# Score products of 128 rows through zero-padded low parts, and constants padded to 64-byte steps, in a four-layer float32 kernel

## The chip, the cores and the metric

The kernel runs on one core of one Trainium2 chip. The metric is device time in microseconds of one execution; the median of three runs is given, with the lowest and the highest. A profile of one further execution shows the instructions of every engine: TensorE (PE; its weight loads are PEld), VectorE (DVE), ScalarE (ACT), GpSimd (POOL), and the DMA queue of SyncE (SP).

## The reference

Four layers work on x, 512 positions of 1024 features, in float32. Layer 1 is stick-breaking attention with 16 heads of 64, layer 2 an HGRN2 mixer with 8 heads of 128, each followed by an MLP with squared ReLU of width 4096. The second block has two layers, each with a gated linear attention branch (4 heads) and a differential attention branch (4 heads, two maps of 64 features each). What the change touches are the scores of both kinds of attention:

```python
# layer 1: q, k are normalised per head of 64 features
z = jnp.einsum('bhqd,bhkd->bhqk', q[:, :, t0:t1], k[:, :, :t1]) * scale
...
# second block: two maps m of 64 features each for a head
s = jnp.einsum('bqhmd,bkhmd->bhmqk', qi, k)
p = jax.nn.softmax(jnp.where(mask, s, -jnp.inf), axis=-1)
attn = p[:, :, 0] - lam * p[:, :, 1]
```

Queries come in blocks of 128, and block t sees the keys up to its own end.

## The kernel before

All activations lie transposed, features on the 128 partitions, positions along the free axis: x0 to x7 are the eight 128-feature chunks of x, 512 columns each. A float32 operand of a projection is held in two parts, a high part h rounded to the short format float32r and a low part l = a - h, so a product a*b is three float32r matmuls: h with wh, l with wh, h with wl, all summed in one PSUM bank. xh and xl are the parts of the normalised x, hh and hl those of other activations (attention outputs, the MLP's hidden layer), wh and wl those of a weight tile, split on the chip from raw, which a DMA fills.

A list of jobs (`job_list`) gives the order: the projections of layer 1 pair by pair (query, key, value of two heads at a time), its output projection, the first MLP, the HGRN projections, their output, the second MLP, then the two layers of the second block. A job of kind T (`job_t`, L558) loads a 128-column weight tile eight times as the stationary operand and streams the 512 positions of hh/hl or xh/xl past it: 24 matmuls of 128x512. A job of kind V (`job_v`, L596) has xh or xl stationary and streams the weights: 96 matmuls. `job_pair` (L532) does the last two output chunks of a phase in halves of 256 columns. All matmuls are issued through `pe` (L400).

The order of instructions on each engine is fixed at build time by a planner, the class `Sched` (L62): every operation has a cost in ns, a thread of work has a priority by its job, and the planner lets a model of the four engines run and appends each operation to its engine where the model dispatches it. The matmul costs are the last entry of each tuple given to `pe`. Buffers are slots in pools: an `Alloc` waits in the model until a slot is free. hh and hl have nine slots each, Q twelve, C, S and A three each. A copy may go to ScalarE or VectorE, whichever the model has free first; subtractions and products go to VectorE; the causal selections of layer 1 (L933) go to GpSimd.

Keys and queries of two heads lie on 64 partitions each of one tile. `headnorm` (L819) normalises the tile, splits it into a high part a and a low part l, and builds for the queries two tiles, one for each head, whose 128 rows hold the head's high part and its low part. For the keys it makes two tiles that hold the head's high part twice, (a, b), and keeps l, with the low parts of both heads on their 64 partitions. `scores` (L881) then takes two matmuls for each query block: one of 128 rows, (q high, q low) with (k high, k high), and one of 64 rows, q high with k low, on the partitions of the head. Head 0's high query part lies on partitions 0 to 63 and head 1's on 64 to 127. Query blocks come in three units (`UNITS`, L867): blocks 0 and 2 together (256 and 384 columns), block 3 (512), block 1 (256). There are 32 issues of each unit: 2 heads or maps of 8 pairs in layer 1 and of 4 heads in each of the two layers of the second block. `sb_elem` (L936) and `d_map` (L1272) issue them; `used` (L871) gives the slots back after the sixth issue.

The constants are laid out in the order in which `const` is called. Each starts at a multiple of 32 bytes of its partition: sv (764 bytes), cst, msk, wgk, neg, kc (32 bytes), x0 to x7, xh, xl, mods, gp, lbt, Rt, rtok, lamt, lp (16 bytes), qbd, onr, then raw, wh, wl and the slots. In this layout x, xh, xl, mods, gp, lbt and Rt start 32 bytes past a multiple of 64; qbd, onr, raw, wh, wl and all slots (hh, hl, Q, C, S, A, v) start at one.

Of the kernel before, what the change touches and what calls it, by code (L numbers as in the profile page):

```python
# [9 lines left out]
F32 = mybir.dt.float32  # L10
# [200 lines left out]
def _fsize(ap):  # L211
    n = 1
    for d in ap.shape[1:]:
        n *= d
    return n
# [75 lines left out]
def block_kernel(ctx: ExitStack, tc, xt, blob, ada, crow_d, sv_d, wgk_d, consts_d, masks_d, out):  # L291
# [7 lines left out]
    def const(name, shape, dtype=F32):  # L299
        return cp.tile(list(shape), dtype, name=name)  # L300
# [3 lines left out]
    msk = const("msk", (128, 4, 32), U8)  # L304
    wgk = const("wgk", (128, 2, 256), F32R)
    neg = const("neg", (64, 64))
    kc = const("kc", (128, 8))
    x = [const(f"x{k}", (128, T)) for k in range(NK)]
    xh = [const(f"xh{k}", (128, T), F32R) for k in range(NK)]
    xl = [const(f"xl{k}", (128, T), F32R) for k in range(NK)]  # L310
# [3 lines left out]
    Rt = const("Rt", (128, T))  # L314
    rtok = const("rtok", (128, 4))
    lamt = const("lamt", (128, 2, 4))
    lp = const("lp", (64, 4))
    ident, ones = cst[:, 0], cst[:, 1]
    one = ones[:, 0:1]
    qbd = const("qbd", (128, 8, 2, 64))  # L320
# [28 lines left out]
    def release(h, l):  # L349
        R.free("hh", h)  # L350
        R.free("hl", l)
# [17 lines left out]
    def tt(out, a, b, op):  # L369
        n = _fsize(out)  # L370
        c = [("DVE", n / 0.96 + 69, lambda: V.tensor_tensor(out=out, in0=a, in1=b, op=op))]  # L371
        return Op(c)
# [27 lines left out]
    def pe(mms, nowait=False):  # L400

        def f():
            for o, a, b, st, sp, _ in mms:
                PE.matmul(o, lhsT=a, rhs=b, start=st, stop=sp)  # L404
        return Op([("PE", sum(m[5] for m in mms), f)], nowait)
# [126 lines left out]
    def job_pair(j, banks, half):  # L532

        role = jobs[j][5]
        l = PAIRS[role]
        evs = operand(role)
        R.spawn(last_chunks(l, banks, j * P - 2), j * P - 2)
        ws = [(yield ev_w[half]), None]
        for i in range(2):
            r = slice(256 * i, 256 * i + 256)  # L540
            for c in range(2):
                if ws[c] is None:
                    ws[c] = yield ev_w[half + 1]
                wh, wl = ws[c]
                o = banks[c][:, r]
                ns = 3 + 256 / 2.4
                for k in range(NK):
                    hh, ll = yield evs[k]
                    a, b = wh[:, k * 128:(k + 1) * 128], wl[:, k * 128:(k + 1) * 128]
                    yield pe([(o, a, hh[:, r], k == 0, False, ns), (o, a, ll[:, r], False, False, ns),  # L550
                              (o, b, hh[:, r], False, k == NK - 1, ns)], nowait=k < NK - 1)
                R.set(ev_done[l, c, i])
                if i:
                    R.free("w", ws[c])
        for k in range(NK):
            release(*evs[k].value)

    def job_t(j, bank, half):  # L558
        role = jobs[j][5]
        w = yield ev_w[half]  # L560
        wh, wl = w
        evs = operand(role)
        split = role == ("wout", 1, NK - 1)
        for r in (slice(0, T // 2), slice(T // 2, T)) if split else (slice(0, T),):
            c = bank[:, r]
            ns = 3 + _fsize(c) / 2.4
            for k in range(NK):
                h, l = yield evs[k]
                a, b = wh[:, k * 128:(k + 1) * 128], wl[:, k * 128:(k + 1) * 128]
                yield pe([(c, a, h[:, r], k == 0, False, ns), (c, a, l[:, r], False, False, ns),  # L570
                          (c, b, h[:, r], False, k == NK - 1, ns)], nowait=k < NK - 1)
            if split and r.start == 0:
                R.spawn(evac[role[0]](j, bank, *role[1:]), (j - AHEAD[role[0]]) * P)
        R.free("w", w)
        last = role[0] == "wo" or role[0] == "wout" or role[0] == "w2"
        if last and role[-1] == NK - 1:
            for k in range(NK):
                release(*evs[k].value)
        if split:
            R.set(ev_last)  # L580
        else:
            R.spawn(evac[role[0]](j, bank, *role[1:]), (j - AHEAD[role[0]]) * P)

    def job_lr(j, bank, half):

        wh, _ = w = yield ev_w[half]
        evs = operand(jobs[j][5])
        for k in range(NK):
            h, l = yield evs[k]
            a = wh[:, k * 128:k * 128 + 64]  # L590
            mms = [(bank[0:64], a, h, k == 0, k == NK - 1, 216), (bank[0:32], a[:, 0:32], l, False, False, 216)]
            yield pe(mms if k == 0 else mms[::-1], nowait=k < NK - 1)
        R.free("w", w)
        R.spawn(e_lr(j, bank, *jobs[j][5][1:]), (j - AHEAD["lr"]) * P)

    def job_v(j, banks, half):  # L596
        role = jobs[j][5]
        evs = operand(role)
        evs2 = [ev_x2[role[1], k] for k in range(NK)] if role[0] == "dv" else evs
        m = 2 if role[0] == "dv" else 1  # L600
        for hf in range(0, 4, m):
            ws = [None] * m
            for n in range(4 * m):
                first, kk = n < 2 * m, n % (2 * m)
                if ws[kk // 2] is None:
                    ws[kk // 2] = yield ev_w[half + hf + kk // 2]
                wh, wl = ws[kk // 2]
                k = hf * 2 + kk
                h, l = yield (evs if first else evs2)[k]
                c = slice(kk % 2 * 512, kk % 2 * 512 + 512)  # L610
                a, b = wh[:, c], wl[:, c]
                done = not first and kk % 2
                for t in (0, 1) if first else (2, 3):
                    th, tl = h[:, t * 128:(t + 1) * 128], l[:, t * 128:(t + 1) * 128]
                    yield pe([(banks[t], th, a, k == 0, False, 216), (banks[t], th, b, False, False, 216),
                              (banks[t], tl, a, False, k == NK - 1, 216)], nowait=not done or t < 3)
                if done:
                    R.free("w", ws[kk // 2])
        for t in range(4):
            R.spawn(evac[role[0]](j, banks[t], *role[1:], t), (j - AHEAD[role[0]]) * P + t)  # L620
# [168 lines left out]
    def sums(out, a, w, tag="A"):  # L789

        if in_areas[0]:
            tags = "N", "N"
            h, l = yield Alloc("N", 2, F32R)
        else:
            tags = "C", "S"
            h = yield Alloc("C", dtype=F32R)
            l = yield Alloc("S", dtype=F32R)
        yield copy(h, a, sbuf=True)
        yield tt(l, a, h.bitcast(F32), ALU.subtract)
        if tag:  # L800
            R.free(tag, a)
        yield pe([(out, w, h, True, False, 216), (out, w, l, False, True, 216)])
        R.free(tags[0], h)
        R.free(tags[1], l)

# [13 lines left out]
    def headnorm(src, gain, bias, tag, is_key, done):  # L819

        a, b, l = yield Alloc(tag, 3, F32R)
        sq = yield Alloc("A")
        yield act(sq, src, AF.Square)
        s = yield Alloc("S")
        p = yield Alloc("tp")
        yield from sums(p, sq, bones_r)
        yield act(s, p, AF.Ln, scale=1.0 / 64, bias=EPSC)  # L830
        R.free("tp", p)
        yield act(s, s, AF.Exp, scale=-0.5, bias=bias)
        yield stt(s, src, gain, s, ALU.mult, ALU.mult)
        done()
        yield copy(a, s, sbuf=True)
        yield tt(l, s, a.bitcast(F32), ALU.subtract)
        R.free("S", s)
        top, bot = slice(0, 64), slice(64, 128)
        yield [copy(b[bot], a[bot], sbuf=True), copy(b[top], a[bot] if is_key else l[bot], sbuf=True)]
        yield copy(a[bot], a[top] if is_key else l[top], sbuf=True)  # L840
        if is_key:
            return (a, b), l
        R.free(tag, l)
        return a, b

# [25 lines left out]
    def used(tag, qn, kn):  # L871

        n = left.setdefault(id(qn), [6, qn])
        n[0] -= 1
        if n[0] == 0:
            R.free(tag, *qn, *kn[0], kn[1])

    def width(unit):
        return sum((qb + 1) * 128 for qb, _ in unit)

    def scores(z, qn, kn, hd, unit):  # L881

        q, (kh, kl) = qn[hd], kn
        r = slice(64 * hd, 64 * hd + 64)
        mms = []
        for qb, off in unit:
            n = (qb + 1) * 128
            w = max(n, 256)
            qc = slice(qb * 128, qb * 128 + 128)
            zo = z[:, off:off + w]  # L890
            mms.append((zo, q[:, qc], kh[hd][:, 0:w], True, False, w / 2.4 + 2))
            mms.append((zo, q[r, qc], kl[r, 0:w], False, True, w / 2.4 + 2))
        return pe(mms)

    def to_keys(src, w, tag, exp=False):
# [441 lines left out]

    def g_decay(l, i, glr):
        p = yield Alloc("z")
        yield pe([(p, wgk[:, l, 128 * i:128 * i + 128], glr, True, True, 216)])  # L1340
        bg = col("bgk", 2 * l + i)
        a = yield Alloc("A")
        yield act(a, p, AF.Abs, bias=bg)
# [339 lines left out]
```

## Time and profile before

| | |
|---|---|
| median of 3 runs | 1844.5 us (1840.95 to 1848.59) |
| profiled execution | 1843.46 us, its span 1841.4 us |
| TensorE | 1812.9 us busy (98%), 9421 matmuls |
| VectorE | 1302.5 us busy (71%) |
| ScalarE | 907.6 us busy (49%) |
| GpSimd | 55.3 us busy (3%) |

The span runs from the first instruction to the last. Layer 1's attention takes until some 262 us, its MLP until 660, HGRN until 930, its MLP until 1320, and the second block's two layers the rest. A matmul's row in the profile spans its whole passage through the engine, so that two neighbours overlap; the step from one start to the next one's is what a matmul costs the engine when nothing waits.

### The profile page before, as it was taken

Reading aid. Unit: us, or ns where it says so; the run is one execution under the profiler, and the core shown is the slowest. Engines: PE = TensorE matmul, PEld = TensorE weight load, DVE = VectorE, ACT = ScalarE, POOL = GpSimd, SP = SyncE. Lnnn points to the kernel's source line nnn. Section 1 sums busy time; section 2 is a strip of 40 time slices with the busy share of each in tenths; the row PEclk is TensorE's granted clock in tenths of the full one; section 3 lists DMA queues with packets and bytes.
Section 4 is the critical chain, followed back from the end, with each engine's and each line's share of the span. In section 5 each row is a group of like instructions: output and inputs, shape, how many; then the busy total and the mean of one; then the engine's idle time right before and its main releaser. Section 6 shows DMA issues by size and latency. Waiting matters only on the chain.

```text
span 1841.4 us, 24301 instructions
## 1 busy us (share of the span) xinstructions
PE 1812.9 (98%) x9421; PEld 1424.6 (77%) x9421; DVE 1302.5 (71%) x2213; ACT 907.6 (49%) x1636; POOL 55.3 (3%) x109
## 2 busy tenths in 40 slices
PE   9999999999999999898999999999999999999999
PEld 6777678888888887676778888888877778877877
DVE  7888877986444569889965353535678886698883
ACT  5778764212222337677742122212458774377771
POOL 0212220000000000000000000000000000000000
PEclk9999999999999999899999999999999999999999
DMA  5111114894222221211222322232222122222122
GB/s 169 61 54 48 57 39 172 300 319 162 96 92 95 100 92 47 70 63 54 69 93 91 102 94 91 95 100 92 92 69 81 58 69 91 92 70 69 58 69 80
DMA packets 49843, 175.53 MB, mean 95 GB/s; under 512 B 5536, under 2 KB 6304, under 8 KB 49728
## 3 DMA queue, kind: packets, MB, share of 16 engines
q1 hardware_dynamic: 49728, 173.99, 28.2%
q8 instruction: 73, 1.20, 0.3%
q14 instruction: 42, 0.34, 0.1%
HBM read 171.87 MB, written 2.10 MB: 94 GB/s over the span
## 4 chain that ended last, share of the span: by engine, by line
PE 90%; DVE 5%; issue 4%; ACT 1%; POOL 0%; POOLq 0%; DVEq 0%
PE bank L404 88%; PE bank L413 2%; DVE wl L371 1%; DVE C L396 1%; DVE S L371 0%; DVE S L376 0%; DVE Q L396 0%; DVE C L371 0%; DVE Q L371 0%; DVE v L376 0%; ACT A L367 0%; ACT big L387 0%; DVE hl L371 0%; DVE xl L376 0%; POOL S L933 0%
## 5 line engine op out<-in xcount | busy, mean ns | idle before, releaser
L404 PE MATMUL bank<-xh,wh 128*128 128x512 f32 (+1 forms) x1296 | 530.3, 409 | 2.2 <-ACT xh L367 1.6
L404 PE MATMUL bank<-xl,wh 128*128 128x512 f32 (+1 forms) x1296 | 513.0, 396 | 0.0
L404 PE MATMUL bank<-xh,wl 128*128 128x512 f32 x1280 | 507.3, 396 | 0.4 <-DVE wl L371 0.4
L371 DVE TENSOR_TENSOR wl<-raw,wh 128x1024 fp32r<-128x1024 f32 (+1 forms) x273 | 332.6, 1218 | 19.5 <-ACT wh L387 15.8
L387 ACT CAST wh<-raw 128x1024 fp32r<-128x1024 f32 x160 | 168.0, 1050 | 342.0 <-PE bank L404 301.8
L404 PE MATMUL bank<-hh,wh 128*128 128x512 f32 (+1 forms) x808 | 308.0, 381 | 2.3 <-DVE hh L389 1.4
L404 PE MATMUL bank<-hh,wl 128*128 128x512 f32 (+1 forms) x808 | 306.3, 379 | 1.6 <-DVE wl L371 1.6
L404 PE MATMUL bank<-hl,wh 128*128 128x512 f32 (+1 forms) x808 | 306.2, 379 | 0.2 <-DVE hl L371 0.2
L404 PEld LDWEIGHTS bank<-xh,wh 128*128 128x128 f32 (+1 forms) x1296 | 243.3, 188 | 69.0 <-issue 8.2
L404 PEld LDWEIGHTS bank<-xh,wl 128*128 128x128 f32 x1280 | 240.8, 188 | 60.4 <-DVE wl L371 2.1
L404 PEld LDWEIGHTS bank<-xl,wh 128*128 128x128 f32 (+1 forms) x1296 | 243.2, 188 | 53.2 <-DVE xl L376 1.2
L371 DVE TENSOR_TENSOR x<-x,bank 128x512 f32<-128x512 f32 (+1 forms) x82 | 55.2, 674 | 183.0 <-PE bank L404 182.6
L404 PEld LDWEIGHTS bank<-hh,wh 128*128 128x128 f32 x808 | 152.0, 188 | 32.0 <-DVE hh L389 1.8
L404 PEld LDWEIGHTS bank<-hh,wl 128*128 128x128 f32 x808 | 152.0, 188 | 31.1 <-DVE wl L371 2.4
L404 PEld LDWEIGHTS bank<-hl,wh 128*128 128x128 f32 x808 | 152.0, 188 | 28.8 <-DVE hl L371 0.5
L367 ACT ACTIVATE S<-A 128x512 f32<-128x512 f32 x64 | 40.5, 633 | 259.7 <-DVE A L376 259.6
L376 DVE SCALAR_TENSOR_TENSOR A<-bank,Rt 128x512 f32<-128x512 f32 x64 | 44.2, 691 | 122.9 <-PE bank L404 122.7
L367 ACT ACTIVATE A<-A 128x512 f32<-128x512 f32 (+1 forms) x220 | 126.9, 595 | 1.7
L389 DVE CAST wh<-raw 128x1024 fp32r<-128x1024 f32 (+1 forms) x115 | 77.8, 677 | 37.6 <-PE bank L404 31.9
L404 PE MATMUL bank<-Q,Q 64*128 64x256 f32 (+5 forms) x256 | 91.2, 407 | 0.0
L404 PEld LDWEIGHTS bank<-Q,Q 128*128 128x128 f32 (+1 forms) x256 | 47.4, 185 | 37.8 <-issue 24.0
L404 PE MATMUL bank<-big,v 128*64 128x128 f32 (+4 forms) x544 | 67.9, 306 | 2.2 <-ACT big L387 2.1
(208 smaller groups left out, 2152.0 us busy)
## 6 DMA issues: line engine op xcount, KB each, us to landing
raw<-blob SPq DMA_DIRECT2D x273, 512.0 KB, 3.5
big<-ada SPq DMA_DIRECT2D x48, 512.0 KB, 4.7
x<-xt SPq DMA_DIRECT2D x8, 256.0 KB, 6.9
out<-x SPq DMA_DIRECT2D x7, 256.0 KB, 2.0
raw<-blob SPq DMA_DIRECT2D x2, 256.0 KB, 4.7
big<-crow SPq DMA_DIRECT2D x1, 512.0 KB, 4.7
out<-x SPq DMA_DIRECT2D x2, 128.0 KB, 1.7
cst<-consts SPq DMA_DIRECT2D x1, 128.0 KB, 6.4
```

The costliest lines, as they stand in the source:

```text
L367: return Op([("ACT", d, lambda: S.activation(out=out, in_=in_, func=func, scale=scale, bias=bias, **kw))])
L371: c = [("DVE", n / 0.96 + 69, lambda: V.tensor_tensor(out=out, in0=a, in1=b, op=op))]
L376: lambda: V.scalar_tensor_tensor(out=out, in0=a, scalar=s, in1=b, op0=op0, op1=op1))])
L387: c.append(("ACT", 0.833 * n + (51 if in_.space == PSUM else 93), lambda: S.copy(out, in_)))
L389: c.append(("DVE", n / (1.92 if sbuf else 0.96) + 68, lambda: V.tensor_copy(out, in_)))
L396: V.tensor_tensor_scan(out=o, data0=one.to_broadcast(list(i.shape)), data1=i, initial=0.0, op0=ALU.mult, op1=ALU.add)
L404: PE.matmul(o, lhsT=a, rhs=b, start=st, stop=sp)
L413: PE.transpose(p[:, b * 128:(b + 1) * 128], src[:, b * 128:(b + 1) * 128], ident)
```

## The change

Keys: `headnorm` takes an hh slot and an hl slot at its start, and GpSimd clears partitions 64 to 127 of the one and 0 to 63 of the other. The subtraction that made l on 128 partitions becomes two on 64 partitions each, one into each slot, so that each holds one head's low part and zeros on the other head's partitions. The two high tiles (a, b) are made as before, but their slots are taken after the norm. `scores` uses the padded slots with the whole 128-row query tile for both matmuls; the zeros take away the query's low part and leave q high with k low. `used` gives the hh and hl slots back. Queries are built as before.

Constants: kc grows from 32 to 64 bytes, lp from 16 to 64. Rt, x, xh, xl, mods, gp and lbt move by 32 bytes, to multiples of 64, and what lies behind lp moves by 64.

Planner: the cost of a matmul is N/2.4 + 13 ns instead of N/2.4 + 3 (or + 2 in the scores), 227 instead of 216 where it is a number. The diff, without the repeated changes of that number:

```diff
-    kc = const("kc", (128, 8))
+
+    kc = const("kc", (128, 16))
...
-    lp = const("lp", (64, 4))
+    lp = const("lp", (64, 16))
...
-                ns = 3 + 256 / 2.4
+                ns = 13 + 256 / 2.4
...
-            ns = 3 + _fsize(c) / 2.4
+            ns = 13 + _fsize(c) / 2.4
...
-        yield pe([(out, w, h, True, False, 216), (out, w, l, False, True, 216)])
+        yield pe([(out, w, h, True, False, 227), (out, w, l, False, True, 227)])
...
-        a, b, l = yield Alloc(tag, 3, F32R)
+        top, bot = slice(0, 64), slice(64, 128)
+        if is_key:
+            ls = []
+            for t_, z_ in (("hh", bot), ("hl", top)):
+                ls.append((yield Alloc(t_, dtype=F32R)))
+                yield Op([("POOL", 460.0, lambda o=ls[-1][z_]: G.memset(o.bitcast(F32), 0.0))], True)
         sq = yield Alloc("A")
...
         done()
+        if is_key:
+            a, b = yield Alloc(tag, 2, F32R)
+            yield copy(a, s, sbuf=True)
+            yield [tt(l[r], s[r], a[r].bitcast(F32), ALU.subtract) for l, r in zip(ls, (top, bot))] + [
+                copy(b[r], a[bot], sbuf=True) for r in (top, bot)]
+            R.free("S", s)
+            yield copy(a[bot], a[top], sbuf=True)
+            return (a, b), tuple(ls)
+        a, b, l = yield Alloc(tag, 3, F32R)
         yield copy(a, s, sbuf=True)
         yield tt(l, s, a.bitcast(F32), ALU.subtract)
         R.free("S", s)
-        top, bot = slice(0, 64), slice(64, 128)
-        yield [copy(b[bot], a[bot], sbuf=True), copy(b[top], a[bot] if is_key else l[bot], sbuf=True)]
-        yield copy(a[bot], a[top] if is_key else l[top], sbuf=True)
-        if is_key:
-            return (a, b), l
+        yield [copy(b[bot], a[bot], sbuf=True), copy(b[top], l[bot], sbuf=True)]
+        yield copy(a[bot], l[top], sbuf=True)
...
-            R.free(tag, *qn, *kn[0], kn[1])
+            R.free(tag, *qn, *kn[0])
+            release(*kn[1])
...
-        q, (kh, kl) = qn[hd], kn
-        r = slice(64 * hd, 64 * hd + 64)
+        q, kh, kl = qn[hd], kn[0][hd], kn[1][hd]
...
-            mms.append((zo, q[:, qc], kh[hd][:, 0:w], True, False, w / 2.4 + 2))
-            mms.append((zo, q[r, qc], kl[r, 0:w], False, True, w / 2.4 + 2))
+            mms.append((zo, q[:, qc], kh[:, 0:w], True, False, w / 2.4 + 13))
+            mms.append((zo, q[:, qc], kl[:, 0:w], False, True, w / 2.4 + 13))
```

## Rows read from the trace of the kernel before

**Rows 1.** The page: busy time of the engines, and the chain of work that ended last, as shares of the span by engine.

```profile
PE 1812.9 (98%) x9421; PEld 1424.6 (77%) x9421; DVE 1302.5 (71%) x2213; ACT 907.6 (49%) x1636; POOL 55.3 (3%) x109
...
PE 90%; DVE 5%; issue 4%; ACT 1%; POOL 0%; POOLq 0%; DVEq 0%
```

**Rows 2.** Busy time of each engine in stretches of the span: the stretch, its length, then busy us and instructions of each engine, TensorE's granted clock, the share of the DMA engines and GB/s. In order: first attention, first MLP, HGRN, and the attention stages of the second block's two layers.

```profile
12.00:262.00 250.00, 247.91 (x1296) 180.55 (x1297) 213.12 (x357) 185.09 (x349) 50.36 (x96) 1.00 0.19 62
...
300.00:660.00 360.00, 360.00 (x1568) 293.45 (x1567) 229.89 (x315) 94.31 (x130) 3.85 (x4) 1.00 0.49 167
700.00:900.00 200.00, 185.29 (x1655) 137.92 (x1654) 180.65 (x391) 143.91 (x268) 0.00 (x0) 0.94 0.19 62
1345.00:1510.00 165.00, 165.00 (x804) 126.84 (x803) 142.91 (x285) 125.72 (x264) 0.00 (x0) 1.00 0.21 67
1595.00:1765.00 170.00, 170.00 (x819) 130.63 (x818) 140.90 (x280) 122.55 (x259) 0.00 (x0) 1.00 0.20 66
```

**Rows 3.** Matmuls of the whole span grouped by operands and shape: output and inputs, rows * stationary columns, moving shape, count, then busy us and mean ns of one, and idle time before them. The moving operand is named first, the stationary one second.

```profile
L404 PE MATMUL bank<-xh,wh 128*128 128x512 f32 x1280 | 524.2, 410 | 2.2 <-ACT xh L367 1.6 <-DVE wh L389 0.6
...
L404 PE MATMUL bank<-wh,xh 128*128 128x512 f32 x128 | 52.3, 409 | 0.0
...
L404 PE MATMUL bank<-Q,Q 64*128 64x256 f32 x64 | 24.4, 381 | 0.0
...
L404 PE MATMUL bank<-Q,Q 64*128 64x512 f32 x32 | 15.9, 497 | 0.0
...
L404 PE MATMUL bank<-Q,Q 64*128 64x384 f32 x32 | 14.1, 440 | 0.0
```

**Rows 4.** Timeline of TensorE near the end of the first attention: start in us, duration, operation, count. Score matmuls (Q,Q) that follow one another are merged into one row with the first one's shape; eight are two issues of the first unit, two are one issue of another unit. hh, hl are the output projection's.

```profile
242.85 2.79 PE L404 MATMUL bank<-Q,Q 128*128 128x256 f32 x8
245.56 0.66 PE L404 MATMUL bank<-big,v 128*64 128x128 f32 x8
246.15 0.93 PE L404 MATMUL bank<-Q,Q 128*128 128x512 f32 x2
247.01 0.50 PE L404 MATMUL bank<-hh,wh 128*128 128x512 f32 x1
247.35 0.40 PE L404 MATMUL bank<-hl,wh 128*128 128x512 f32 x1
247.58 0.40 PE L404 MATMUL bank<-hh,wl 128*128 128x512 f32 x1
247.81 0.82 PE L404 MATMUL bank<-Q,Q 128*128 128x512 f32 x2
248.57 0.50 PE L404 MATMUL bank<-hh,wh 128*128 128x512 f32 x1
248.91 0.39 PE L404 MATMUL bank<-hl,wh 128*128 128x512 f32 x1
249.14 0.40 PE L404 MATMUL bank<-hh,wl 128*128 128x512 f32 x1
...
250.07 0.39 PE L404 MATMUL bank<-hh,wh 128*128 128x512 f32 x1
...
250.75 0.39 PE L404 MATMUL bank<-hh,wh 128*128 128x512 f32 x1
...
252.79 0.59 PE L404 MATMUL bank<-Q,Q 128*128 128x256 f32 x2
253.30 0.50 PE L404 MATMUL bank<-hh,wh 128*128 128x512 f32 x1
253.64 0.40 PE L404 MATMUL bank<-hl,wh 128*128 128x512 f32 x1
```

**Rows 5.** The same view a little later: projection matmuls behind four transposes (cst,C).

```profile
254.10 0.60 PE L413 MATMUL bank<-cst,C 128*128 128x128 f32 x4
254.46 0.48 PE L404 MATMUL bank<-hh,wh 128*128 128x512 f32 x1
254.77 0.40 PE L404 MATMUL bank<-hl,wh 128*128 128x512 f32 x1
255.01 0.40 PE L404 MATMUL bank<-hh,wl 128*128 128x512 f32 x1
```

**Rows 6.** The same view in the first MLP, from the first to the last of seven matmuls in a row with xh or xl moving; and in the V job before HGRN, from the first to the last of sixteen in a row with xh or xl stationary.

```profile
600.23 0.40 PE L404 MATMUL bank<-xh,wh 128*128 128x512 f32 x1
...
601.63 0.40 PE L404 MATMUL bank<-xh,wh 128*128 128x512 f32 x1
...
676.17 0.40 PE L404 MATMUL bank<-wh,xh 128*128 128x512 f32 x1
...
679.67 0.40 PE L404 MATMUL bank<-wh,xh 128*128 128x512 f32 x1
```

**Rows 7.** The same view at the end of the second MLP, from the first to the last of thirteen matmuls in a row of 256 columns with 128 rows.

```profile
1302.74 0.28 PE L404 MATMUL bank<-hh,wh 128*128 128x256 f32 x1
...
1304.17 0.28 PE L404 MATMUL bank<-hh,wh 128*128 128x256 f32 x1
```

**Rows 8.** Groups by line, with busy us and mean ns of one: the subtraction that makes a low part in the first attention, on VectorE, and a clear on GpSimd at the program's start.

```profile
L371 DVE TENSOR_TENSOR Q<-S,Q 128x512 fp32r<-128x512 f32 x16 | 10.9, 680 | 0.1
...
L1584 POOL MEMSET qbd<- 128x768 f32 x1 | 0.7, 737 | 0.0
```

**Rows 9.** Timeline of TensorE at the start of HGRN: a matmul that waited, with the idle time before it and what ended it in brackets.

```profile
742.39 0.64 PE L404 MATMUL bank<-S 128*32 128x32 f32 x16 [5.24 <-DVE S L371]
```

More of the change, by code (lines that the diff above doesn't have):

```diff
@@ L590, in job_lr @@
             a = wh[:, k * 128:k * 128 + 64]
-            mms = [(bank[0:64], a, h, k == 0, k == NK - 1, 216), (bank[0:32], a[:, 0:32], l, False, False, 216)]
+            mms = [(bank[0:64], a, h, k == 0, k == NK - 1, 227), (bank[0:32], a[:, 0:32], l, False, False, 227)]
             yield pe(mms if k == 0 else mms[::-1], nowait=k < NK - 1)
@@ L614, in job_v @@
                     th, tl = h[:, t * 128:(t + 1) * 128], l[:, t * 128:(t + 1) * 128]
-                    yield pe([(banks[t], th, a, k == 0, False, 216), (banks[t], th, b, False, False, 216),
-                              (banks[t], tl, a, False, k == NK - 1, 216)], nowait=not done or t < 3)
+                    yield pe([(banks[t], th, a, k == 0, False, 227), (banks[t], th, b, False, False, 227),
+                              (banks[t], tl, a, False, k == NK - 1, 227)], nowait=not done or t < 3)
                 if done:
@@ L1339, in g_decay @@
         p = yield Alloc("z")
-        yield pe([(p, wgk[:, l, 128 * i:128 * i + 128], glr, True, True, 216)])
+        yield pe([(p, wgk[:, l, 128 * i:128 * i + 128], glr, True, True, 227)])
         bg = col("bgk", 2 * l + i)
```

## The prediction

> **What bounds the kernel now.** I read the page first: TensorE is busy 98% of the span, and 90% of the chain that ended last is TensorE [rows 1]. A busy matmul row says little by itself, since matmuls overlap, so the second view is the stages: in the first attention (12 to 262 us), in the first MLP (300 to 660) and in the two attention stages of the second block (1345 to 1510, 1595 to 1765) TensorE has 2.1, 0, 0 and 0 us without a matmul; only the HGRN stage (700 to 900) shows 14.7 us without one, and there VectorE is busy 180.65 of 200 us [rows 2]. So outside HGRN the time is the sum of the steps from one matmul's start to the next one's, and what the change does to these steps is what it does to the time, until another engine becomes late. The third view is therefore the timeline of TensorE alone: I read starts, not durations.
>
> **Scores: what the 64-row products cost.** Each score is a pair: a 128-row product and a 64-row product, 64 pairs of 256 columns, 32 of 384 and 32 of 512 [rows 3], in 96 issues of three kinds (2 heads, 16 pairs or heads of layers, 3 units). From the starts [rows 4]: two issues of the first unit (256, 256, 384, 384 columns each) take 242.85 to 245.56, 1.355 us each. One of the second unit (512, 512) takes 0.86 (246.15 to 247.01, behind fp32 products) or 0.76 (247.81 to 248.57, behind a projection); I take 0.81. One of the third unit (256, 256) takes 0.51 behind a projection; behind fp32 products I estimate 0.10 more, as for the second unit, and take 0.56. Behind a 64-row product the next projection matmul takes 0.34 (247.01 to 247.35, 248.57 to 248.91, 253.30 to 253.64) where its neighbours take 0.23: 0.105 more. I count that for 60 of the 96 issues, since some are followed by another score, which has it in its own price. Sum: 32 x (1.355 + 0.81 + 0.56) + 60 x 0.105 = 87.2 + 6.3 = 93.5 us.
>
> With 128 rows everywhere: a 256-column product with 128 rows takes 0.119 (1302.74 to 1304.17 for 12 steps) [rows 7], a settled 512 takes 0.227 (250.07 to 250.75 for 3 steps) [rows 4], 384 lies between at 0.173. In broken streams they take up to 0.235 [rows 4, 5], so I add 0.004 to each: units of 0.60, 0.462 and 0.246, 32 x 1.308 = 41.9. A first product behind transposes takes 0.31 instead of 0.23 [rows 5]; that stays, for a third of the issues 32 x 0.08 = 2.6. After: 44.5. **Saved: 49 us**, 24.5 in the first attention and 12.25 in each later one. Lower end, with the cheap readings of every unit and no step behind: 32 x 2.625 - 44.5 = 39.5. Upper end, with the dear ones and all 96 steps behind: 32 x 2.825 + 10 - 41.9 = 58.5.
>
> The Trainium skill, "TensorEngine Tiling (Array Packing)", Key Properties, says that a change of the tiling mode drains TensorE; the trace agrees, with 0.34 beside 0.23 at the change. The same page, When to Use Tiling, speaks against this change: a contraction of 64 rows should be tiled, so that two products run side by side, and padding would then cost what it had saved. By that the saving would be nothing or below; in the trace no two score products start side by side, so the sum goes by the starts.
>
> **Alignment.** The program's layout puts x, xh, xl and Rt 32 bytes past a 64-byte step (kc's 32 bytes lie ahead of them), while hh, hl, wh, wl and Q begin on one. In the MLP xh and xl take 1.40 us for 6 steps, 0.2333 each, and where xh is the stationary operand and wh moves, 3.50 us for 15 steps, again 0.2333 [rows 6]; settled hh takes 0.2267 [rows 4]. Behind an interruption hh also takes 0.23 to 0.24 and needs some seven matmuls to settle [rows 4, 5]. 1280 xh,wh matmuls stand for 3 x 1280 = 3840, and 128 for 3 x 128 = 384 with xh or xl stationary [rows 3]. The MLPs hold 2 x 32 x 24 = 1536 of them in long runs: 1536 x 0.0067 = 10.2 us. The other 2688 are in streams broken by scores and transposes: between 0 and 18 us, I take half, 9.0 (1.9 in the first attention, 2.6 in HGRN, 2.25 in each later stage). **Saved: 19 us**, ends 10 and 28.
>
> **What is added.** Per key (16 of them): one more subtraction on VectorE, 512 columns on 64 partitions instead of on 128. The full one takes 0.680 us [rows 8], and I take the same, since the columns are the same: 16 x 0.68 = 10.9 us, 5.4 of it in the first attention. Two clears on GpSimd: one of 768 columns took 0.737 [rows 8], so some 0.5 each, 16 us in all on an engine that is busy 50 of 250 us in the first attention and 0 later [rows 2]. Behind a clear that waits for its slot's last reader stand the causal selections, and behind those the scans; a selection that comes 0.5 us late is hidden by the several units in flight, and without that cover it would be 16 x 0.5 = 8 us. A key gives up one Q slot and holds an hh and an hl slot from before its norm until its sixth score. The longer costs told to the planner (13 for 3, 227 for 216) issue nothing; they reorder. A better order can regain at most the 2.1 idle us of the first attention; a worse one I bound by HGRN's 14.7 [rows 2], and take 0. lp's padding only keeps the later tiles on their steps.
>
> **What is late next.** TensorE alone: 49 + 19 = 68 us. The sum is made against the profiled execution, 1843.5 us (span 1841.4 and 2 around it; the median of the runs, 1844.5, is 1 above): 1775.5. But VectorE comes close: in the first attention 213.1 + 5.4 = 218.5 us of work for 250 - 26.4 = 223.6 us of TensorE, 98%; in the second block's stages 145.6 of 150.5 (97%) and 143.6 of 155.5 (92%) [rows 2]. It is 87% now with no TensorE idle time, and 90% in HGRN with 14.7 us of it, in waits like the 5.24 us one for VectorE's S [rows 9]. I take 95% as what VectorE can reach: 230.0 and 153.3 us, so 6.4 + 2.8 us are not got, and HGRN keeps its 2.6. 1775.5 + 11.8 = **1787**, rounded up by the one microsecond to the median: 1788.
>
> **The rivals.**
> - TensorE stays the bound everywhere (20%): ScalarE, busy 185 of 250 [rows 2], takes casts from VectorE, and nothing is lost: 1775.
> - The offset isn't what makes xh slower (10%). For it: hh behind an interruption has the same pace as xh. Against it: that pace ends after some seven matmuls and xh's doesn't within the MLP. Then only the scores count, and VectorE's limit takes 5 us of them: 1843.5 - 49 + 5 = 1799. The Trainium skill, "SBUF — State Buffer", Door 1, would have it so: it gives SBUF 16-byte lines, and an offset of 32 is on such a line. Its rule agrees with none of the 0.2333 rows.
> - VectorE gets no further than the 90% of HGRN (10%): 242.8, 161.8 and 159.6 us for the three stages, 19.2 + 11.3 + 4.1 + 2.6 = 37 us lost: 1812.
> - Slower: the nine hh and hl slots (3%). Results of the first attention hold up to eight until the output projection, two keys in flight take two more. Each key that must wait for a slot delays its pair by one norm chain, some eleven steps of 0.68 us, 7.5 us. If all 16 waited, 120 us, less the 56 gained: 1907. It decides from 8 waiting keys on; by the count of slots only the last pair or two can wait.
> - The edit doesn't do what it says (3%): zero-padded products keep the high step for a reason that isn't their rows. Against it: the same steps appear nowhere but beside 64-row and fp32 products. Then 1843.5 - 19 + 2.6 = 1827.
> - My forecast, 1788: 54%.
>
> **How the numbers follow.** The range takes in the first four faster cases and the ends of the scores' saving next to them: 1768 to 1813. A measurement of this kernel can tell about 0.5% (9 us) from no change; all but the slot case and a sliver lie below 1835: faster 0.95, same 0.02, slower 0.03.
>
> **What would show it.** In the trace after: no 64-row product; an issue of the second unit near 0.46 us instead of 0.76 to 0.86, and the projection matmul behind it near 0.23; xh at 0.227 in the MLP (wrong if still 0.233); the MLP stage shorter by 5 us. The first attention should end some 20 us earlier, with VectorE near 95% and first TensorE waits for VectorE of a microsecond or less; waits of several microseconds, or on GpSimd clears, would make the forecast wrong upward, and no waits at all downward.

## The result and the profile after

The changed kernel takes 1787.41 us (median of 4 runs, 1786.54 to 1789.65) beside 1844.01 for the kernel before (4 runs, 1840.95 to 1848.59): a ratio of 0.9693, 95% interval 0.9671 to 0.9715. The forecast was 1788. The sum came out right; two of its six stages did not, and their misses happened to cancel.

The page of the kernel after, busy time by engine and the chain that ended last by engine, to be held against [rows 1]:

```profile
PE 1747.4 (98%) x9421; PEld 1413.1 (79%) x9421; DVE 1310.3 (73%) x2231; ACT 901.1 (50%) x1634; POOL 70.9 (4%) x141
...
PE 71%; DVE 20%; DMA 3%; ACT 3%; issue 2%; POOL 0%; SPq 0%; POOLq 0%; DVEq 0%; ACTq 0%
```

TensorE still shows 98% busy, but its share of the chain fell from 90% to 71% and VectorE's rose from 5% to 20%. This is a hint that the bound has begun to move, and not a measure of it: in the first MLP a third of the chain runs over other engines, although TensorE is without a matmul there for only 0.8 of 352 us, and a faster kernel below (no_costs) has 85% and 11%. The waits, stage by stage, tell more.

The timeline of TensorE after, near the end of the first attention: two issues of the second unit (512 columns), the projection matmul behind them, and, after the dots, the first and the last of seven matmuls in a row with xh or xl moving in the first MLP:

```profile
235.06 0.39 PE L405 MATMUL bank<-Q,Q 128*128 128x512 f32 x1
235.30 0.40 PE L405 MATMUL bank<-hh,Q 128*128 128x512 f32 x1
235.53 0.40 PE L405 MATMUL bank<-Q,Q 128*128 128x512 f32 x1
235.76 0.39 PE L405 MATMUL bank<-hl,Q 128*128 128x512 f32 x1
235.99 0.39 PE L405 MATMUL bank<-hh,wh 128*128 128x512 f32 x1
236.22 0.40 PE L405 MATMUL bank<-hl,wh 128*128 128x512 f32 x1
...
560.61 0.39 PE L405 MATMUL bank<-xh,wh 128*128 128x512 f32 x1
...
561.97 0.39 PE L405 MATMUL bank<-xh,wh 128*128 128x512 f32 x1
```

An issue takes 0.47 us (235.06 to 235.53), where it took 0.76 to 0.86 [rows 4]; the matmul behind takes 0.23 instead of 0.34. Six steps of xh take 1.36 us, 0.2267 each, where they took 1.40 [rows 6]. Summed over the steps that begin with a score product, 256 of them, the whole came down from 86.2 to 49.5 us; 2.8 of the 49.5 are in steps over 0.45 us, beyond the first 0.3, which are waits.

Where the time came from, by stage. I took the stages' ends from the timeline: the start of the last projection matmul of the output projection, of the MLP and so on (us; "attn 1" to its output projection, HGRN likewise, "layer 3" and "layer 4" are the second block's):

```
              attn 1    MLP 1     HGRN    MLP 2  layer 3  layer 4     span
before         294.6    353.9    311.0    355.0    261.8    265.1   1841.4
after          285.9    350.0    298.4    350.1    248.9    251.4   1784.7
gained           8.7      3.9     12.6      4.9     12.9     13.7     56.7
forecast        20.0      5.1      0.0      5.1     11.7     14.5     56.4
```

The stretches of after that answer to [rows 2] (first attention, HGRN, layers 3 and 4; columns as there), and TensorE's two largest groups of waits in the first attention, with who ended them: us in total, times, longest:

```profile
12.00:253.00 241.00, 227.93 (x1294) 175.44 (x1294) 220.99 (x370) 178.45 (x346) 55.23 (x107) 0.99 0.19 65
687.00:877.00 190.00, 182.19 (x1674) 138.48 (x1673) 182.00 (x402) 143.42 (x271) 0.00 (x0) 0.98 0.19 63
1315.00:1467.00 152.00, 151.18 (x803) 123.51 (x803) 139.88 (x283) 126.89 (x268) 0.78 (x2) 1.00 0.22 70
1552.00:1708.00 156.00, 155.06 (x807) 126.37 (x806) 137.54 (x280) 122.92 (x259) 0.00 (x0) 1.00 0.23 71
```

```profile
PE bank L414 <- DVE C L372: 4.7, 8, 1.0
PE bank L414 <- POOL C L945: 4.3, 6, 1.7
```

In the first attention TensorE is now without a matmul for 13.1 of 241 us (2.1 of 250 before), 9.0 of them at the transposes (L414), waiting for the work of VectorE and GpSimd that makes C; VectorE is busy 92%. In this stretch the chain that ended last is 57% VectorE and 30% TensorE (12% and 63% before), so here the bound has moved. In layers 3 and 4 it is still 76% TensorE, which is without a matmul for less than 1 us in each. HGRN is the surprise: 7.8 us without a matmul in its stretch instead of 14.7, and VectorE at 96%.

### The profile page after: what moved, and what is told of

It reads as the page before. It is cut to its first block, busy times and chain, and to the rows that moved or that the text cites. A ratio compares the mean times of both kernels' runs of the same rounds, so it can differ in the third digit from the quotient of the medians.

```text
span 1784.7 us, 24336 instructions
## 1 busy us (share of the span) xinstructions
PE 1747.4 (98%) x9421; PEld 1413.1 (79%) x9421; DVE 1310.3 (73%) x2231; ACT 901.1 (50%) x1634; POOL 70.9 (4%) x141
## 4 chain that ended last, share of the span: by engine, by line
PE 71%; DVE 20%; DMA 3%; ACT 3%; issue 2%; POOL 0%; SPq 0%; POOLq 0%; DVEq 0%; ACTq 0%
PE bank L405 69%; DMA big<-ada 3%; DVE wl L372 3%; DVE C L397 2%; DVE C L372 2%; DVE S L377 2%; DVE S L372 2%; DVE big L1068 1%; DVE Q L372 1%; PE bank L414 1%; ACT S L368 1%; DVE Q L397 1%; ACT A L368 1%; DVE wh L390 1%; DVE hl L372 1%
## 5 line engine op out<-in xcount | busy, mean ns | idle before, releaser
L405 PE MATMUL bank<-xh,wh 128*128 128x512 f32 (+1 forms) x1296 | 518.7, 400 | 3.4 <-ACT xh L368 2.5
L405 PE MATMUL bank<-xl,wh 128*128 128x512 f32 (+1 forms) x1296 | 506.4, 391 | 0.1
L405 PE MATMUL bank<-xh,wl 128*128 128x512 f32 x1280 | 500.9, 391 | 0.6 <-DVE wl L372 0.5
L372 DVE TENSOR_TENSOR wl<-raw,wh 128x1024 fp32r<-128x1024 f32 (+1 forms) x273 | 332.1, 1217 | 17.4 <-ACT wh L388 13.2
L390 DVE CAST wh<-raw 128x1024 fp32r<-128x1024 f32 (+1 forms) x118 | 83.3, 706 | 31.8 <-PE bank L405 26.2
L405 PE MATMUL bank<-big,v 128*64 128x128 f32 (+4 forms) x544 | 63.7, 298 | 1.0 <-ACT big L368 0.5
L405 PEld LDWEIGHTS bank<-big,v 128*64 128x64 f32 (+1 forms) x544 | 49.1, 159 | 18.9 <-issue 6.4
L368 ACT ACTIVATE A<-bank 128x512 f32<-128x512 f32 (+1 forms) x80 | 43.6, 553 | 29.3 <-PE bank L405 22.1
```

The costliest lines, as they stand in the source:

```text
L368: return Op([("ACT", d, lambda: S.activation(out=out, in_=in_, func=func, scale=scale, bias=bias, **kw))])
L390: c.append(("DVE", n / (1.92 if sbuf else 0.96) + 68, lambda: V.tensor_copy(out, in_)))
```

## The experiments

Each kernel was timed against the kernel before on the same chip; ratios are to it. A line of the table of stages, as above, for the kernels that the text rests on:

```
              attn 1    MLP 1     HGRN    MLP 2  layer 3  layer 4     span
pad_only       296.4    348.6    306.3    349.7    260.3    262.3   1823.6
scores_only    277.3    353.9    310.8    355.0    250.6    253.6   1801.2
costs_only     297.9    353.8    300.5    355.4    262.1    264.9   1834.6
no_costs       276.3    348.6    306.7    349.8    247.6    250.6   1779.6
hgrn_costs     275.5    348.6    297.8    349.8    247.6    250.7   1770.0
sub_twice      295.8    349.7    297.2    350.1    253.7    256.3   1802.8
sub_on_pool    289.7    348.6    305.0    349.8    254.0    256.0   1803.1
told_true      289.3    348.6    325.0    349.8    252.3    256.0   1821.0
```

**The three parts, each alone.**

The padding of the constants (pad_only):

```diff
-    kc = const("kc", (128, 8))
+    kc = const("kc", (128, 16))
...
-    lp = const("lp", (64, 4))
+    lp = const("lp", (64, 16))
```

> The kernel before with kc and lp padded, nothing else; the planner's costs are the old ones, so every engine's order is that of before. Offset theory (an operand 32 bytes past a 64-byte step costs a 512-column matmul 0.2333 instead of 0.2267 us): the MLP's xh steps fall to 0.227, the two MLP stages to 5 us less each, and of the 2688 matmuls in broken streams about half the saving comes, 9 us: 1825, between 1816 and 1834. Rival (the offset is not the cause): xh stays at 0.233 and the time at 1844.

Measured: 1824.5 us, ratio 0.990 (0.9882 to 0.9917), 16.7 us less than the 1841.21 beside it. The MLPs got 5.3 us shorter each; HGRN 4.7, layers 3 and 4 1.5 and 2.8; while the first attention was 1.8 us longer, which no run explains. So the second term of the sum, 19 us, was 17.

The scores alone (scores_only): the padded slots as in the change, `kc`, `lp` and the planner's costs as before.

```diff
-            mms.append((zo, q[:, qc], kh[hd][:, 0:w], True, False, w / 2.4 + 2))
-            mms.append((zo, q[r, qc], kl[r, 0:w], False, True, w / 2.4 + 2))
+            mms.append((zo, q[:, qc], kh[:, 0:w], True, False, w / 2.4 + 2))
+            mms.append((zo, q[:, qc], kl[:, 0:w], False, True, w / 2.4 + 2))
```

> The scores and the keys' padded slots as after, but kc and lp and the planner's costs as before. Theory of the prediction: TensorE saves 49 us, VectorE's limit takes some 5 of them: 1800. Rival (the order matters more: the planner still believes a score pair costs half of what it did on the chip and a projection matmul 216 ns): more than 15 us of the 49 go into waits of TensorE for VectorE, 1810 or more.

Measured: 1801.46 us, ratio 0.9776 (0.9759 to 0.9792), 39.8 us less. The first attention gained 17.3 us, layers 3 and 4 11.2 and 11.5, the rest nothing. The rival's reading, a loss of over 15 us of the 49, is not met; 9 are missing, of which some 4 were never there, since the steps give a saving of 45 (see below).

The planner's costs alone (costs_only):

```diff
-                ns = 3 + 256 / 2.4
+                ns = 13 + 256 / 2.4
...
-            ns = 3 + _fsize(c) / 2.4
+            ns = 13 + _fsize(c) / 2.4
...
-            mms.append((zo, q[:, qc], kh[hd][:, 0:w], True, False, w / 2.4 + 2))
-            mms.append((zo, q[r, qc], kl[r, 0:w], False, True, w / 2.4 + 2))
+            mms.append((zo, q[:, qc], kh[hd][:, 0:w], True, False, w / 2.4 + 13))
+            mms.append((zo, q[r, qc], kl[r, 0:w], False, True, w / 2.4 + 13))
```

and 227 for 216 everywhere.

> The kernel before with the planner's costs of matmuls as after, nothing else. Theory of the prediction: the order moves no work, 1844 within 3 us. Rival (HGRN, which got 16 us shorter after, owes that to another order): HGRN ends some 10 us earlier and the time is near 1834.

Measured: 1836.99 us, ratio 0.9969 (0.9957 to 0.9982). HGRN gained 10.5 us, the first attention lost 3.3. HGRN's stretch in this kernel, to be held against its line in [rows 2]:

```profile
700.00:900.00 200.00, 193.45 (x1781) 146.25 (x1780) 191.45 (x420) 152.30 (x286) 0.00 (x0) 0.98 0.20 64
```

TensorE is without a matmul for 6.5 instead of 14.7 us, VectorE is busy 191 instead of 181, and the granted clock is 0.98 instead of 0.94. The work is that of before, but not all of it is on the same engine, as the page of this kernel shows beside [rows 1] (x2213 on VectorE, x1636 on ScalarE):

```profile
PE 1813.3 (99%) x9421; PEld 1426.3 (78%) x9421; DVE 1308.6 (71%) x2234; ACT 897.5 (49%) x1615; POOL 52.4 (3%) x109
```

A copy goes to ScalarE or VectorE, whichever the planner's model has free first, and with the new costs 21 copies went from ScalarE to VectorE, six of them in HGRN. The rival is right: HGRN's gain comes from what the planner was told. VectorE, the busier of the two, got more to do there, so the gain is put down to the order rather than to the copies; no run holds one fixed and changes the other. (The expectation's 16 us for HGRN after are 12.6 in the table of stages.)

**The offset: which one counts.** kc padded and lp not puts x, xh and xl on a 64-byte step and everything behind lp, wh, wl, hh and hl among it, 32 bytes past one.

```diff
-    lp = const("lp", (64, 16))
+    lp = const("lp", (64, 4))
```

> The kernel after with lp back at 16 bytes: x, xh and xl begin on a 64-byte step, and hh, hl, wh, wl and all slots 32 bytes past one. Offset theory, either operand: every float32r matmul of 512 columns takes 0.233, also xh, whose stationary wh is off; 6312 x 0.0067 = 42 us more on TensorE, less what waits hide: 1815 to 1829. Only the moving operand counts: xh at 0.227, hh at 0.233, 16 us more, 1803. Offset not the cause: 1787.

> The same program as the kernel with kc at 64 and lp at 16 bytes, once more for a profile at the granted clock of 1.0, since the one taken ran at 0.5 throughout. After its 1803: xh steps 0.227 and hh steps 0.233 in the MLP if only the moving operand's offset counts; both 0.233 if either operand's does.

Measured: 1802.94 and 1802.82 us, ratio 0.9782 (0.9765 to 0.9799). The rows come from the second: the profiled execution of the first took 3509.54 us, with TensorE busy 3493.9 us for the same matmuls, twice the second's 1768.8. It is not in the ratio, and its trace holds no record of the granted clock, so the expectation's 0.5 is not shown. The time is the one expected if the moving operand alone counted, but the rows say otherwise. Timeline of the second run in the first MLP, six steps of xh and xl, then fifteen of hh and hl:

```profile
560.75 0.39 PE L405 MATMUL bank<-xh,wh 128*128 128x512 f32 x1
...
562.15 0.39 PE L405 MATMUL bank<-xh,wh 128*128 128x512 f32 x1
...
599.91 0.39 PE L405 MATMUL bank<-hh,wh 128*128 128x512 f32 x1
...
603.31 0.39 PE L405 MATMUL bank<-hh,wh 128*128 128x512 f32 x1
```

xh, which is on a step, takes 1.40 us for six, 0.2333; hh, which is off, takes 3.40 for fifteen, 0.2267. Both readings that I had written down fall. What fits all rows is that the moving and the stationary operand must lie alike: wh is off too, so hh lies like it and xh doesn't. In the kernel before it was the other way round, with the V jobs (xh stationary, wh moving) slow as well [rows 6]. The test is a layout in which all of these are off alike (lp_alone, the change with kc at its old 32 bytes):

```diff
-    kc = const("kc", (128, 16))
+    kc = const("kc", (128, 8))
```

> The kernel after with kc back at 32 bytes: x, xh, xl and everything behind lp begin 32 bytes past a 64-byte step, all of them alike. Theory formed from the run with kc padded and lp not, where xh on a step took 0.2333 with wh off one, and hh took 0.2267 with both off: the offset of the moving operand against the stationary one counts, not the step itself. Then xh and hh both take 0.2267 in the MLPs and the time is after's, 1787 within 3 us. The offset theory of the prediction (a step missed by either operand costs) gives 0.2333 everywhere and 1815 to 1829; with the moving operand alone likewise 0.2333 for xh and hh.

Measured: 1788.93 us, ratio 0.9704 (0.9687 to 0.972), as after. Its timeline in the first MLP, six steps of xh and xl, then nine of hh and hl:

```profile
560.18 0.39 PE L405 MATMUL bank<-xh,wh 128*128 128x512 f32 x1
...
561.54 0.39 PE L405 MATMUL bank<-xh,wh 128*128 128x512 f32 x1
...
599.62 0.39 PE L405 MATMUL bank<-hh,wh 128*128 128x512 f32 x1
...
601.66 0.39 PE L405 MATMUL bank<-hh,wh 128*128 128x512 f32 x1
```

1.36 for six and 2.04 for nine: 0.2267 both, with every operand 32 bytes past a step. So what counts is not the 64-byte step but the difference between the two operands.

**VectorE and GpSimd: what is late now.** Both half subtractions of a key done twice, in the same order (sub_twice):

```diff
-            yield [tt(l[r], s[r], a[r].bitcast(F32), ALU.subtract) for l, r in zip(ls, (top, bot))] + [
+            yield [Op([("DVE", tt(l[r], s[r], a[r].bitcast(F32), ALU.subtract).choices[0][1], lambda l=l, r=r: [
+                V.tensor_tensor(out=l[r], in0=s[r], in1=a[r].bitcast(F32), op=ALU.subtract) for _ in range(2)])])
+                for l, r in zip(ls, (top, bot))] + [
```

> The kernel after with both half subtractions of a key done twice, at the old price to the planner, so the order is the same: 2 x 16 x 0.68 = 21.8 us more work on VectorE, 10.9 in the first attention, 5.4 in each later stage. If VectorE sets the pace of these stages now, most of it shows: 15 us or more. If its work is hidden, as the prediction took it to be below 95%, under 6 us.

Measured: 1808.01 us, ratio 0.9809 (0.9784 to 0.9834), some 20 us over after. Of 10.9 us of added work in the first attention 9.9 show, of 5.4 in layers 3 and 4 4.8 and 4.9. So the subtractions lie on the path that sets the time in all three stages once they are doubled: in this kernel's trace 20.8 of their 21.9 us in the first attention are on the chain that ended last, and 10.9 of 11.0 in each later stage. Whether it is VectorE's load or the longer chain of a key that costs the time, this run doesn't separate. In the first attention 65% of the chain is VectorE's, 17.8 us of weight splits among it, which are no part of a key's chain: that speaks for the load, at a busy share of 92%. In layers 3 and 4 VectorE's part of it is 38%, with the doubled subtractions almost whole: there the key's chain explains the loss as well.

The clears done twice, in the same order (clears_twice):

```diff
-                yield Op([("POOL", 460.0, lambda o=ls[-1][z_]: G.memset(o.bitcast(F32), 0.0))], True)
+                yield Op([("POOL", 460.0, lambda o=ls[-1][z_]: (G.memset(o.bitcast(F32), 0.0), G.memset(o.bitcast(F32), 0.0)))], True)
```

> The kernel after with each of the keys' clears on GpSimd done twice, at the old price to the planner, so the order is the same: 32 x 0.55 = 17.5 us more on GpSimd, half of it in the first attention, where the causal selections stand behind them. If the clears are hidden, as the prediction had it, 1787 to 1790; if the selections behind them are late for TensorE, up to 8 us more, 1795, all of it in the first attention.

Measured: 1789.39 us, ratio 0.9703 (0.9685 to 0.972), within 2 us of after. The clears are hidden.

The subtractions on GpSimd, with the planner's old costs (sub_on_pool), beside the same kernel with them on VectorE (no_costs, below):

```diff
-            yield [tt(l[r], s[r], a[r].bitcast(F32), ALU.subtract) for l, r in zip(ls, (top, bot))] + [
+            yield [Op([("POOL", 1000.0, lambda l=l, r=r: G.tensor_tensor(
+                out=l[r], in0=s[r], in1=a[r].bitcast(F32), op=ALU.subtract))]) for l, r in zip(ls, (top, bot))] + [
```

> The kernel after with the planner's old matmul costs, and both half subtractions of a key on GpSimd instead of VectorE, told to the planner as 1000 ns each. If VectorE sets the pace of the attention stages, taking 16 x 2 x 0.68 = 21.8 us from it gives back 10 to 20 us on the 1780 of the same kernel with these on VectorE: 1760 to 1770. If GpSimd's own queue, where the causal selections stand behind, is as late as VectorE, or the longer chain of a key counts, 1778 or more.

Measured: 1806.05 us, ratio 0.9797 (0.9781 to 0.9812), 26 us over no_costs: a miss. Groups by line of this kernel, the subtractions on GpSimd over the whole span and two casts on VectorE in layer 3, with busy us, mean ns of one, and idle time before:

```profile
L844 POOL TENSOR_TENSOR hh<-S,Q 64x512 fp32r<-64x512 f32 x16 | 26.2, 1636 | 502.6 <-ACT Q L388 267.6 <-DVE Q L390 235.0
...
L390 DVE CAST wh<-raw 128x1024 fp32r<-128x1024 f32 x14 | 11.4, 813 | 6.0 <-PE bank L405 5.9
...
L390 DVE CAST Q<-Q 64x512 fp32r<-64x512 f32 x12 | 8.4, 703 | 2.2 <-POOL hl L844 1.9
```

One takes 1.64 us (1.48 into hl), not 1.0, and VectorE's casts beside it take 0.703 and 0.813 us where layer 3 of the kernel before has

```profile
L389 DVE CAST wh<-raw 128x1024 fp32r<-128x1024 f32 x11 | 7.6, 691 | 5.7 <-PE bank L404 5.4
...
L389 DVE CAST Q<-Q 64x512 fp32r<-64x512 f32 x8 | 3.4, 424 | 0.2
```

Of VectorE's casts of 64x512 over the whole span, the 12 that overlapped a GpSimd subtraction took 1.08 us on average, and the 22 that overlapped no GpSimd instruction 0.42. The Trainium skill, "SBUF — State Buffer", Who interferes with whom, says that VectorE and GpSimd share a pair of SBUF ports that one holds for a whole instruction; the longer casts agree with it. Engines' busy time over the span, in this kernel and then in no_costs:

```profile
PE 1751.0 (97%) x9421; PEld 1416.8 (79%) x9421; DVE 1308.9 (73%) x2183; ACT 902.0 (50%) x1650; POOL 126.6 (7%) x173
...
PE 1744.1 (98%) x9421; PEld 1416.5 (80%) x9421; DVE 1301.5 (73%) x2210; ACT 910.9 (51%) x1655; POOL 73.3 (4%) x141
```

Some 21.8 us of subtractions left VectorE, and yet it is busy 7.4 us longer. So this run didn't relieve VectorE and can't tell what that would bring. How much of the 26 us is slower casts and how much the longer chain of a key was not separated.

**The order.** The change without the planner's new costs (no_costs):

```diff
-            ns = 13 + _fsize(c) / 2.4
+            ns = 3 + _fsize(c) / 2.4
```

and so for the others.

> The kernel after with the planner's old matmul costs (3 and 216): padded scores and padded constants alone. The parts add up: 16.7 and 39.7 us off, 1785 beside 1841. The first attention is then shorter than after by the 3 us that the new costs alone added to it (7.6 more, then 4.3 less), HGRN longer by some 11. Rival (the new costs and the new scores belong together, since a planner that takes a score for half its price orders the rest badly): 1795 or more.

Measured: 1780.16 us, ratio 0.9655 (0.9634 to 0.9676), faster than the change as it was made (0.9693, 0.9671 to 0.9715; the intervals overlap by 0.0005). The first attention is 9.6 us shorter than after, HGRN 8.3 longer. Its chain over the span, and its stretches of the first attention and of layer 3:

```profile
PE 85%; DVE 11%; ACT 2%; issue 1%; POOL 0%; DMA 0%; SPq 0%; POOLq 0%; DVEq 0%
...
12.00:247.00 235.00, 228.23 (x1315) 178.80 (x1314) 215.62 (x362) 185.70 (x358) 57.56 (x108) 0.99 0.20 66
1315.00:1467.00 152.00, 151.72 (x805) 125.21 (x804) 139.95 (x282) 129.15 (x273) 0.52 (x1) 1.00 0.21 69
```

Here too the kernels differ by more than the order: 21 copies that after has on VectorE are on ScalarE, nine of them in the first attention, where VectorE has 5.5 us less to do. How much of the 9.6 us is these copies and how much the order was not separated. In layers 3 and 4 the stages now gain 14.2 and 14.5 us, and TensorE is without a matmul for 0.3 us of layer 3's stretch. The parts don't add up: alone the new costs took 4 us off, on top of the other two parts they add some 5 to 7.

All costs on VectorE and ScalarE set to what the trace shows (told_true):

```diff
-        c = [("DVE", n / 0.96 + 69, lambda: V.tensor_tensor(out=out, in0=a, in1=b, op=op))]
+        c = [("DVE", n / 0.96 + 147, lambda: V.tensor_tensor(out=out, in0=a, in1=b, op=op))]
...
-        return Op([("DVE", sum(_fsize(o) / 0.96 + 69 for o, _ in segs), f)])
+        return Op([("DVE", sum(_fsize(o) / 0.48 + 155 for o, _ in segs), f)])
```

and so for the other operations.

> The kernel after, with the planner's costs on ScalarE and VectorE set to what the trace of before shows: 147 to 215 ns over the columns on VectorE instead of 69 to 130, 160 to 200 on ScalarE instead of 51 to 93, and scans at 1/0.48 ns a column instead of 1/0.96. Nothing else. If the first attention lost its gain to an order that takes VectorE for faster than it is, TensorE's waits there fall from some 14 us to under 7, and the time to 1780 or less. If VectorE's work itself is the limit, the time stays within 3 us of after, 1784 to 1790.

Measured: 1820.87 us, ratio 0.9874 (0.9853 to 0.9896), 33 us worse than after: neither expectation. HGRN alone lost 26.6 us. TensorE's two largest groups of waits in the whole span:

```profile
PE bank L405 <- DVE S L372: 15.6, 10, 6.3
PE bank L405 <- DVE wl L372: 10.8, 5, 4.3
```

Truer prices gave a worse plan. Which of the planner's choices did the harm I have not found.

The new matmul costs in HGRN's projections and its output projection only, the old ones elsewhere (hgrn_costs):

```diff
-            ns = 13 + _fsize(c) / 2.4
+            ns = (13 if role[0] in ("f", "q", "g") or role[:2] == ("wo", 1) else 3) + _fsize(c) / 2.4
```

> The kernel after with the planner's old matmul costs, except in HGRN's projections and its output projection, where they are the new ones. If the new costs help HGRN (10 us net alone) and hurt the first attention, this has the better of both: 1780 - 8 = 1772, HGRN near 244 us and the first attention near 276. If the order of HGRN depends on all that was ordered before it, rather than on its own costs, HGRN stays near 255 and the time at 1780.

Measured: 1771.61 us, ratio 0.9612 (0.9593 to 0.963): the time is as expected, and shorter than after's and no_costs'. (The expectation's 255 and 244 us for HGRN can't be held against the table of stages, which has 306.7 for no_costs and 297.8 here, 8.9 less.) HGRN keeps the change's 12.6 us and more (13.2), the first attention gains 19.1 instead of 8.7. Its two stretches:

```profile
12.00:245.00 233.00, 226.13 (x1309) 177.03 (x1308) 215.13 (x361) 185.35 (x357) 57.70 (x108) 0.99 0.20 67
675.00:865.00 190.00, 182.63 (x1675) 138.39 (x1674) 181.97 (x401) 143.88 (x272) 0.00 (x0) 0.98 0.19 64
```

The first line is the first attention, the second HGRN. VectorE is busy 92% in the first attention here too, TensorE without a matmul for 6.9 us instead of 13.1.

## Why the prediction was right

- **The scores' steps.** Right, slightly over: 49 us forecast. 86.2 - 49.5 + 2.8 of waits = 39.5, and the steps of the projection matmuls right behind a score, 56 of them at 0.337 before and 0.233 after, add 5.8: 45.3. Most of the difference is on the side of after, 46.7 us for the 44.5 forecast. The rows of after show 0.47 for an issue and 0.23 behind it, as written. Alone, the part brought 39.8 us of time.
- **The offset.** The size was right (19 forecast, 16.7 measured alone, MLPs 5.3 each against 5.1); the cause was not. The prediction put it down to beginning on a 64-byte step; what counts, in the four layouts run, is that the moving and the stationary operand lie alike (0.2267) or 32 bytes apart (0.2333). The diff pads both constants and so makes them alike by the way; lp_alone does it with one. The 16-byte lines of the Trainium skill, "SBUF — State Buffer", Door 1, taken as the ground of a rival, don't tell the layouts apart that ran at 0.2267 and at 0.2333, since 0 and 32 both lie on such a line.
- **VectorE's limit.** The mechanism is borne out for the first attention: TensorE's time without a matmul there rose from 2.1 to 6.8 us with the old costs (no_costs) and to 13.1 with the new ones, where 6.4 us were forecast as not got, and 57% of the chain there is VectorE's in the kernel after. The 95% was a guess and no constant: 92% was reached in the first attention (after 221.0 of 241, no_costs 215.6 of 235, hgrn_costs 215.1 of 233), 96% in HGRN. The 2.8 us forecast as lost in layer 3 were not lost in no_costs, where seven copies of that stage are on ScalarE that were on VectorE before: what the prediction's first rival said, in this stage. Nor did HGRN keep its 2.6 us: it got 4.3 us shorter with the old costs.
- **The planner's costs.** This step failed: "A better order can regain at most the 2.1 idle us of the first attention; a worse one I bound by HGRN's 14.7 [rows 2], and take 0". On top of the other parts the new costs lost 9.6 us in the first attention and won 8.3 in HGRN. Without them the first attention gains 18.3 us, near the 20 forecast. The bound on a better order fell, since HGRN's idle time was left out of it; the bound on a worse one held; the value of 0 held in neither stage. And the costs did more than "reorder": they also moved 21 copies from ScalarE to VectorE. So the forecast of the first attention missed by 11 us and that of HGRN by 12.6, in opposite directions, and that the total came within 1 us was luck.
- **The clears** are hidden, as said. **The slots**: no sign that they ran out, since no stage is longer than before in any kernel with the padded slots and the old costs.
- **Where the gain went.** TensorE got some 62 us less to do (45.3 by the steps of the scores, 16.7 by the time of the padding alone), and the time fell by 56.6. hgrn_costs gets 71 us, more than that; 8.9 of them are HGRN's gain over no_costs.

## What to carry to other kernels

Read the cost of a matmul from the steps between starts, kind by kind and neighbour by neighbour; that gave 64-row products their price, and it is how padding a contraction with zeros can be faster than a smaller one. When a change also alters what a build-time planner believes, time it apart, stage by stage, since it can move a stage by 10 us either way: here by another order and by 21 copies on another engine, with the same work to do. And look at the second engine before the first one is relieved: VectorE, 85% busy in the first attention with TensorE hardly waiting, made up most of the chain there once the stage's TensorE work was some 10% shorter.

## What the hardware showed that I had not expected

- A float32r matmul of 512 columns steps at 0.2267 us when its moving and its stationary operand begin at the same place within 64 bytes, 0 and 0 or 32 and 32, and at 0.2333 when one is 32 bytes off the other, whichever of the two it is.
- A GpSimd subtraction of 64x512 took 1.64 us into hh and 1.48 into hl, a VectorE one 0.68. VectorE's cast of 64x512 took 0.42 us by itself and 1.08 on average where it overlapped such a GpSimd subtraction (sub_on_pool). Twice the clears, 0.55 us each, changed the time by 2 us (clears_twice).
- In layers 3 and 4 of after, VectorE was 92 and 88% busy while TensorE was without a matmul for less than 1 us (151.18 of 152, 155.06 of 156): 5.4 us more work for VectorE in the chains of the keys still cost 4.8 and 4.9.
